# Two half-row stores in place of three stores for the last row block, with its first half scaled by two engines side by side

## Chip, cores, metric

One core of one Trainium2 chip. The metric is the device time of one execution, in microseconds (us). Every ratio below is the mean time of one kernel's fast runs over the mean of the other's fast runs of the same rounds, so it is not quite the ratio of the medians that are quoted. A run is fast when it is within 1.5% of the fastest run of the same kernel. The sets of experiments ran on different chips; a ratio compares runs of one set.

## The reference

```python
m, k, n = 2048, 2048, 2048
def reference(a, b, gamma, eps):
    x = np.matmul(a, b)
    rms = np.sqrt(np.mean(x ** 2, axis=-1, keepdims=True) + eps)
    return (gamma * x / rms).astype(np.float32)
```

The output is 2048 rows of 8 KB. A row can only be scaled when all of it is known, so the last block of 128 rows has a serial end: last matmul, square, root, reciprocal, scale, store.

## The kernel before

The product is computed with a Strassen-like scheme (seven products of half blocks) in 16-bit types. What matters here is the end of the last group of two row blocks, `ra` and `rb`. CH is 512 columns (a quarter of a row, 2 KB), HALF is 1024 (4 KB). `by_r` is a ScalarE ACTIVATE with a scale per row, `scaled_gamma` a VectorE operation.

```python
# ... ra: left quarter by ScalarE, second quarter by GpSimd, right half by VectorE; three stores on nc.sync
right = a_pool.tile([P, K], FP32, name="a32")[:, 0:HALF]
add(right[:, 0:CH], p4[1], gam[2], ALU.mult)
# ... last matmuls into two half banks, their squares, the partial sums
r_b = inverse_rms(half_sq[:, 1:2], part)                       # root on ScalarE, reciprocal on VectorE
nc.vector.tensor_scalar_mul(out=xb[:, 0:CH], in0=xb[:, 0:CH], scalar1=r_b)   # left quarter
nc.sync.dma_start(out=rows(rb, 0, CH), in_=xb[:, 0:CH])
by_r(right[:, 0:CH], r_b)                                      # third quarter
for bank, col in zip(half, halves):
    scaled_gamma(right[:, CH:][:, col], bank, r_b, gam[3][:, col])   # fourth quarter
nc.sync.dma_start(out=rows(rb, HALF, N), in_=right)
by_r(xb[:, CH:], r_b)                                          # second quarter
nc.scalar.dma_start(out=rows(rb, CH, HALF), in_=xb[:, CH:])
```

## Time and profile before

| | |
|---|---|
| time, first three runs | 221.2 us (221.19 to 221.22) |
| profiled span | 219.0 us |
| TensorE busy | 208.8 us, 95% |
| last reciprocal starts | 212.89 us |
| stores of the last block: issue, landing after that start | 0.71, 3.30; 1.53, 4.84; 1.56, 5.01 us |
| from that start to the end ("tail") | 6.11 us |

The lines themselves stand in the prediction. Read them from the end backwards: a closing of 1.1 us, in front of it the landing of the last store, in front of that the bytes. I use the start of the last reciprocal as zero for everything that follows it, since the change can only act after it. A DMA issue is counted from the start of its instruction on the queue; the store "lands" when its semaphore is complete. The time from issue to first packet is called lead, from last packet to landing receipt, from last landing to the end closing. Times of first packets, last packets and landings to a hundredth are read from the trace's packet and semaphore records; the views give landings to a tenth.

### The profile page before, as it was taken

How to read it: one execution, taken by the hardware profiler on the slowest of the kernel's cores; microseconds unless marked ns; L12 is line 12 of the kernel's file. 1: busy time of each engine (PE TensorE's matmuls, PEld its weight loads, DVE VectorE, ACT ScalarE, POOL GpSimd, SP SyncE). 2: the span in 40 equal slices, each digit the busy share in tenths (PEclk: the TensorE clock that was granted, in tenths of full speed). 3: DMA queues.
4: the chain of work that ended last, by engine and by line, in shares of the span. 5: the costliest groups of instructions: out<-in, count | busy, mean ns of one | idle time of the engine just before them, and what ended most of it. 6: DMA issues, size and time to landing. Idle time of an engine off the chain costs nothing.

```text
span 219.0 us, 3023 instructions
## 1 busy us (share of the span) xinstructions
PE 208.8 (95%) x1012; PEld 98.4 (45%) x1032; DVE 165.9 (76%) x326; ACT 127.0 (58%) x263; POOL 36.2 (17%) x75
## 2 busy tenths in 40 slices
PE   7999999999999999999999999999999999999970
PEld 3544544444455444444444444444444444444440
DVE  1228799999899998988794649856794759787781
ACT  2110002920599898788646996289747996334471
POOL 7644433433020002100200002000200000000040
PEclk9999999999999999999999999999999999999996
DMA  7999999999939698939899049955799349145045
GB/s 152 175 202 206 204 206 209 210 208 224 414 91 332 232 278 214 379 153 263 213 294 381 19 87 272 355 233 96 174 291 396 57 89 365 69 178 208 1 179 206
DMA packets 36864, 46.60 MB, mean 213 GB/s; under 512 B 22256, under 2 KB 26352, under 8 KB 35568
## 3 DMA queue, kind: packets, MB, share of 16 engines
q0 software_dynamic: 10608, 23.86, 44.3%
q1 hardware_dynamic: 25824, 22.02, 33.4%
q10 hardware_dynamic: 416, 0.52, 0.7%
q8 instruction: 8, 0.13, 0.2%
q14 instruction: 8, 0.07, 0.1%
HBM read 34.60 MB, written 16.78 MB: 235 GB/s over the span
## 4 chain that ended last, share of the span: by engine, by line
PE 91%; DMA 3%; issue 1%; ACT 1%; POOL 1%; DVE 0%; ACTq 0%; POOLq 0%
PE acc L285 71%; PE acc L388 16%; DMA early<-in_a_dram 3%; PE tbank L419 2%; PE tbank L168 2%; PE acc L799 1%; POOL b L102 0%; PE tbank L185 0%; PE acc L185 0%; ACT x L738 0%; DVE head_at L173 0%; ACT sq L802 0%; ACT rms L352 0%; POOL t_left masks.py:199 0%; POOL t_left masks.py:197 0%
## 5 line engine op out<-in xcount | busy, mean ns | idle before, releaser
L285 PE MATMUL acc<-b,s 128*128 128x512 bf16 x397 | 92.7, 379 | 0.7
L285 PEld LDWEIGHTS <-s 128*128 128x128 f16 (+1 forms) x512 | 50.0, 98 | 59.6 <-DVE s L260 0.2
L388 PE MATMUL acc<-b,head_at 128*128 128x512 bf16 x171 | 42.2, 379 | 0.4 <-DMA b<-in_b_dram 0.3
L303 ACT ACTIVATE sq<-x 128x512 bf16<-128x512 f32 x53 | 33.4, 630 | 6.9 <-DVE x L731 3.0
L370 DVE SCALAR_TENSOR_TENSOR x<-x,r,gamma_sb 128x1024 f32<-128x1024 f32 x28 | 34.9, 1281 | 0.7
L219 ACT ACTIVATE sq<-a 128x1024 bf16<-128x1024 f32 x24 | 25.3, 1053 | 2.0 <-DMA a<-in_a_dram 1.4
L388 PEld LDWEIGHTS <-head_at 128*128 128x128 bf16 x176 | 16.9, 98 | 19.5 <-issue 0.7
L242 ACT ACTIVATE head_at<-a,s 128x2048 f16<-128x2048 f32 x10 | 20.0, 1998 | 3.4 <-DVE s L229 3.3
L102 POOL DMA_DIRECT2D b<-in_b_dram x32 | 17.2, 540 | 20.4 <-DMA b<-in_b_dram 14.1
L430 ACT COPY x<-acc 128x512 f32<-128x512 f32 x5 | 2.9, 582 | 24.6 <-PE acc L388 24.6
L285 PEld LDWEIGHTS <-head_at 128*128 128x128 f16 (+1 forms) x112 | 11.0, 98 | 13.2
L285 PEld LDWEIGHTS <-at_even 128*128 128x128 f16 x96 | 9.4, 98 | 11.3
L285 PE MATMUL acc<-early,head_at 128*128 128x512 bf16 x63 | 14.4, 379 | 0.1
L285 PE MATMUL acc<-early,s 128*128 128x512 bf16 x56 | 14.2, 379 | 0.0
L260 DVE TENSOR_TENSOR s<-head_at 128x1024 f16<-128x1024 f16 (+5 forms) x22 | 13.4, 636 | 0.1
L615 DVE TENSOR_TENSOR x<-x,x 128x512 f32<-128x512 f32 x9 | 6.2, 692 | 8.8 <-ACT x L613 8.3
L127 POOL COPY pace<-x 128x1 f32<-128x1 f32 x4 | 1.7, 413 | 66.3 <-DVE x L624 65.0
L597 ACT COPY x<-acc 128x512 f32<-128x512 f32 x9 | 5.2, 573 | 11.5 <-PE acc L285 7.7
L285 PE MATMUL acc<-t_left,s 128*128 128x512 bf16 x47 | 11.3, 379 | 0.1
L783 POOL TENSOR_SCALAR x<-x,r 128x512 f32<-128x512 f32 x1 | 2.7, 2653 | 51.2 <-DVE r L346 51.2
L276 DVE TENSOR_TENSOR b<-b 128x1024 bf16<-128x1024 bf16 x16 | 10.8, 686 | 0.2
L173 DVE COPY head_at<-tbank 128x1024 bf16<-128x1024 bf16 x7 | 4.8, 692 | 8.0 <-PE tbank L168 7.9
(113 smaller groups left out, 239.3 us busy)
## 6 DMA issues: line engine op xcount, KB each, us to landing
out_dram<-x SPq DMA_DIRECT2D x29, 512.0 KB, 3.7
a<-in_a_dram POOLq DMA_DIRECT2D x10, 1024.0 KB, 8.6
b<-in_b_dram POOLq DMA_DIRECT2D x32, 256.0 KB, 9.9
a<-in_a_dram POOLq DMA_DIRECT2D x4, 512.0 KB, 9.8
early<-in_a_dram POOLq DMA_DIRECT2D x7, 256.0 KB, 10.0
gamma_sb<-in_gamma_dram POOLq DMA_DIRECT2D x2, 512.0 KB, 8.3
out_dram<-x SPq DMA_DIRECT2D x3, 256.0 KB, 2.6
out_dram<-a SPq DMA_DIRECT2D x1, 512.0 KB, 3.3
```

Source lines behind the costliest of these rows:

```text
L102: nc.gpsimd.dma_start(out=raw[j][kp][:, t, :], in_=b[lo:lo + P, j * HALF:(j + 1) * HALF])
L173: nc.vector.tensor_copy(out=head_at[:, 2 * kp:2 * kp + 2, :, :], in_=view)
L219: nc.scalar.activation(out=junk, in_=a32[mb][:, h * HALF:(h + 1) * HALF], func=ACTF.Square, scale=2.0 ** -8, accum_out=n2[:, h:h + 1])
L242: nc.scalar.activation(out=a16[mb], in_=a32.pop(mb), func=ACTF.Copy, scale=factor.pop(mb))
L260: nc.vector.tensor_tensor(out=sum_of(g, s)[:, lo:hi, :], in0=x[:, lo:hi, :], in1=y[:, lo:hi, :], op=op)
L276: nc.vector.tensor_tensor(out=flat[:, 1:3, :], in0=flat[:, 1:3, :], in1=flat[:, 0::3, :], op=ALU.add)
L285: nc.tensor.matmul(bank, lhsT[:, kp, :], rhs, start=(start and kp == 0), stop=(kp == KP - 1), skip_group_check=not start)
L303: nc.scalar.activation(out=sq[:, 0:CH], in_=src, func=ACTF.Square, scale=inv_sqrt_n, accum_out=msq[mb][:, c:c + 1])
L370: nc.vector.scalar_tensor_tensor(out=x, in0=x, scalar=inverse_of[mb], in1=gamma_sb[:, h * HALF:(h + 1) * HALF], op0=ALU.mult, op1=ALU.mult)
L388: nc.tensor.matmul(bank, head_at[:, kt, r, :], head_rhs(c, kt), start=(kt == 0), stop=(kt == KT - 1))
L597: nc.scalar.copy(out=c, in_=one[1])
L615: nc.vector.tensor_tensor(out=t, in0=t, in1=x12, op=ALU.add)
```

## The change

The intent is fewer, larger stores: the left half is finished by two engines at once and goes out as one store of 512 KB, and ScalarE issues no store.

```diff
         nc.vector.tensor_scalar_mul(out=xb[:, 0:CH], in0=xb[:, 0:CH], scalar1=r_b)
-        nc.sync.dma_start(out=rows(rb, 0, CH), in_=xb[:, 0:CH])
+        by_r(xb[:, CH:], r_b)
+        nc.sync.dma_start(out=rows(rb, 0, HALF), in_=xb)
         by_r(right[:, 0:CH], r_b)
         for bank, col in zip(half, halves):
             scaled_gamma(right[:, CH:][:, col], bank, r_b, gam[3][:, col])
         nc.sync.dma_start(out=rows(rb, HALF, N), in_=right)
-        by_r(xb[:, CH:], r_b)
-        nc.scalar.dma_start(out=rows(rb, CH, HALF), in_=xb[:, CH:])
```

## The prediction

> **What bounds the kernel now.** I read the page first (busy shares, then the chain that ended last), then the chain after 208 us, the timeline of the last 6 us, the list of transfers with their landing times, and the DMA rate in quarter microseconds.
>
> ```profile
> PE 208.8 (95%) x1012; PEld 98.4 (45%) x1032; DVE 165.9 (76%) x326; ACT 127.0 (58%) x263; POOL 36.2 (17%) x75
> PE 91%; DMA 3%; issue 1%; ACT 1%; POOL 1%; DVE 0%; ACTq 0%; POOLq 0%
> ```
>
> Matmuls bound the kernel: TensorE is busy for 208.8 of 219.0 us and is 91% of the chain. The change touches nothing that feeds TensorE, so only the time after the last matmul is in play. The chain after 208 us says where that is; its columns are start, length, what:
>
> ```profile
> 210.21 1.76 PE acc L799 x16
> ...
> 212.89 0.17 DVE r L346
> 213.06 0.02 issue
> 213.08 0.03 ACT a L738
> 213.11 0.60 issue
> 213.71 0.70 ACT x L738
> ```
>
> TensorE ends at 211.97. The square, the root and the reciprocal bring 1/rms of the last row block at 213.06. From there to the end, 219.0, is 5.9 us, 2.7% of the span: all that the change can reach, and most of that is a floor. The timeline of that stretch (start, length, engine, line):
>
> ```profile
> 213.08 0.72 ACT L738 ACTIVATE a<-a,r 128x512 f32<-128x512 f32 x1 [0.23 <-DVE r L346]
> 213.09 0.49 DVE L808 TENSOR_SCALAR x<-x,r 128x512 f32<-128x512 f32 x1
> 213.49 0.87 DVE L734 SCALAR_TENSOR_TENSOR a<-acc,r,gamma_sb 128x256 f32<-128x256 f32 x2
> 213.60 0.33 SPq L809 DMA_DIRECT2D out_dram<-x  x1
> 213.71 0.70 ACT L738 ACTIVATE x<-x,r 128x512 f32<-128x512 f32 x1
> 214.42 0.33 SPq L813 DMA_DIRECT2D out_dram<-a  x1
> 214.45 0.36 ACTq L815 DMA_DIRECT2D out_dram<-x  x1
> ```
>
> Three stores leave: 256 KB of the left quarter at 213.60 and, nearly together, 512 KB of the right half at 214.42 (SyncE's queue) and 256 KB of the second quarter at 214.45 (ScalarE's queue). Their times to landing:
>
> ```profile
> out_dram<-a SPq DMA_DIRECT2D x1, 512.0 KB, 3.3
> out_dram<-x ACTq DMA_DIRECT2D x1, 256.0 KB, 3.5
> ```
>
> So the right half lands at 214.42 + 3.3 = 217.7, and the quarter on ScalarE's queue last, at 214.45 + 3.5 = 217.9. The remaining 1.1 us to 219.0 is the closing of the program. What sets 217.9? The DMA rate by quarter microseconds (the last two figures of a row are DMA share and GB/s):
>
> ```profile
> 213.75:214.00 0.25, 0.00 (x0) 0.00 (x0) 0.25 (x2) 0.25 (x2) 0.00 (x0) 1.00 0.10 25
> 214.00:214.25 0.25, 0.00 (x0) 0.00 (x0) 0.25 (x1) 0.25 (x1) 0.00 (x0) 1.00 0.06 16
> 214.25:214.50 0.25, 0.00 (x0) 0.00 (x0) 0.11 (x1) 0.17 (x1) 0.00 (x0) 1.00 0.24 90
> 214.50:214.75 0.25, 0.00 (x0) 0.00 (x0) 0.00 (x0) 0.00 (x0) 0.00 (x0) 1.00 0.99 377
> ...
> 215.00:215.25 0.25, 0.00 (x0) 0.00 (x0) 0.00 (x0) 0.00 (x0) 0.00 (x0) 0.50 0.66 205
> 215.25:215.50 0.25, 0.00 (x0) 0.00 (x0) 0.00 (x0) 0.00 (x0) 0.00 (x0) 0.50 1.08 426
> ```
>
> The engines idle near 214.0 (the block before is out), start at about 214.44 (0.24 of the quarter), and then run full until 217.4, but for one hole: in 215.00 to 215.25 they move 205 GB/s where about 390 would fit, which loses about 0.12 us. There the first 256 KB are out and the next two stores, issued 0.8 us after it, have not begun. So this end is: a first issue, a lead time, 1 MB at the DMA rate, a receipt, the closing. The last ACTIVATE, though the chain names it, is only half of a tie with that queue of bytes.
>
> **What the Trainium skill says.** "DMA: Bandwidth & Descriptors", section "Issuing engines are not separate DMA queues": transfers from SyncE and ScalarE run on the same 16 DMA engines and interleave; a second issuer saves only issue time. The trace agrees: the two stores issued together land within 0.2 us of each other, at one engine set's rate. So dropping ScalarE's queue should cost no bandwidth. The same page, "Latency and other measured facts", gives about 600 ns to first byte on these queues. The trace shows more: 213.60 to 214.44 is 0.84 us, and the store issued at 210.13 began at 210.96, 0.83 us. I use 0.83. "ScalarE: Activation LUTs", section "What ACT_TABLE_LOAD costs": 186 ns + 0.833 ns an element, and about 93 ns for a pointer operand; 512 elements with a pointer scale come to about 706 ns. The trace has 705 to 723 ns.
>
> **The change part by part.**
> - *ScalarE's order.* It scales the second quarter first and the right half's first quarter second. Same two instructions, same lengths: the second quarter is ready at 213.08 + 0.72 = 213.80, the other at about 214.42. No work is added or removed. The built program confirms that only these two change places and one DMA issue goes.
> - *First store.* It is now 512 KB and waits for both engines: VectorE is done at 213.58, ScalarE at 213.80. With the 0.03 us from a ScalarE end to the issue (210.10 to 210.13 for the block before), it goes at 213.83 and not 213.60: **+0.23 us** on the path.
> - *Second store.* The right half needs VectorE (213.49 + 0.87 = 214.36) and ScalarE (214.42): issue at about 214.45, 0.03 later than before. Off the path: the first store's bytes occupy the engines until about 214.66 + 1.3 = 215.95, and this one is ready to stream at 214.45 + 0.83 = 215.28. So the hole at 215.0 disappears.
> - *Third store.* Removed from ScalarE's queue; its bytes ride in the first. 1 MB in all, as before.
>
> How fast does one queue move a pair of half-row stores? The kernel before has a clean pair, issued at 193.9 and 195.1 while no loads run; compared with the present end:
>
> ```profile
> 194.70:197.45 2.75, 2.75 (x13) 1.27 (x13) 2.45 (x6) 1.40 (x4) 0.00 (x0) 1.00 0.94 381
> 214.42:217.41 2.99, 0.00 (x0) 0.00 (x0) 0.00 (x0) 0.00 (x0) 0.00 (x0) 0.58 0.92 351
> ```
>
> The same 1.05 MB take 2.75 us there, 2.99 us here: **-0.24 us** if the new pair is like that pair. It may do a little better, as its second store has more time in hand: at the 400 GB/s of full quarters 1.05 MB take 2.62 us, **-0.37**.
>
> Sum: first byte at 213.83 + 0.83 = 214.66; last byte 2.62 to 2.75 later, 217.28 to 217.41 (before: 217.41); receipt as before, 217.9 - 217.4 = 0.5 us; landing at 217.8 to 217.9. The two terms cancel: +0.23 against -0.24 to -0.37. Net 0.0 to -0.14, middle **-0.1 us**. Closing unchanged at 1.1 us. From the median of 221.2 us, that gives **221.1 us**, a ratio of 0.9995.
>
> **The rivals.**
> 1. *The late start is paid in full.* If the rate were the 351 GB/s of the present end, the 0.23 us would stay: 221.4 us. For it: 1 MB has to follow the first issue in any case, and the idle stretch before it just grows. Against it: the hole at 215.0, which only exists because the first store is short, and the clean pair's 381 GB/s.
> 2. *Fewer issues and one queue bring a real gain.* The old last landing came from ScalarE's queue. If that queue began late and dragged the end, and the receipt shrinks too (the clean pair's second store landed 2.7 us after issue at 195.08, so about 0.35 us after its last byte, against 0.5 here), another 0.15 us goes: 220.9 us. For it: ScalarE's quarter takes 3.5 us to land although it is half the size. Against it: the right half landed only 0.2 us earlier, so the queue can't be blamed for more.
> 3. *A straggler.* Not every late half-row store is clean: of the next pair, issued at 197.5 and 198.7, one took 2.7 and the other 3.4 us to land with no load beside it. A last store that meets this ends 0.7 us late: 221.8 us. For: it happened in one of four such stores. Against: the present three repeats lie within 0.03 us, so it isn't random from run to run, but a changed end may have its own.
>
> None reaches 2%, which is 4.4 us; even all 5.9 us after 1/rms would have to shrink by three quarters.
>
> **Range and chances.** The mechanisms span 220.9 to 221.4 with 221.8 as a tail; repeats differ by 0.03 us, and I allow for another chip or day. Predicted 221.1 us, range 220.8 to 221.5. Within 2%: 0.98; faster by over 2%: 0.01; slower: 0.01.
>
> **What would show it.** In the changed profile: two ACTIVATEs of about 0.71 us back to back from 1/rms, the second quarter first; the first 512 KB store issued about 0.77 us after 1/rms (before: 0.54), the second about 0.62 us after the first; DMA idle until about 1.6 us after 1/rms, then no hole, about 380 to 400 GB/s for some 2.7 us; landings of about 2.7 us for the first and 3.4 us for the second (217.85 - 214.45); a closing of 1.1 us. TensorE and everything before 213 us stay as they are. I am wrong if the hole stays, if the pair runs at 350 GB/s or less, if ScalarE delays the first issue beyond 213.9, or if time moves before the last matmul.

## The result, and the profile after

The changed kernel took 220.87 us (median of 6, 220.70 to 221.83), the kernel before 221.18 us (median of 6, 220.88 to 221.22). The ratio is 0.9995, with a 95% interval of 0.9977 to 1.0013: the same, as far as times can tell. Both spans of the two profiles print as 219.0 us, but their last reciprocals start 0.13 us apart, so the tails differ.

The chain of the changed kernel after the last reciprocal (start, length, what):

```profile
213.02 0.17 DVE r L346
213.20 0.02 issue
213.22 0.72 ACT x L738
213.94 0.61 ACTq L849
```

Two ACTIVATEs in a row ended the old chain. Now the chain names one, then ScalarE's queue at L849, the program's end: it drains until 214.55, when the second ACTIVATE (213.85 + 0.70) is over. So that ACTIVATE still runs; in neither kernel does the chain go on to the transfers. The timeline of the same stretch:

```profile
213.22 0.72 ACT L738 ACTIVATE x<-x,r 128x512 f32<-128x512 f32 x1 [0.23 <-DVE r L346]
213.22 0.49 DVE L808 TENSOR_SCALAR x<-x,r 128x512 f32<-128x512 f32 x1
213.62 0.87 DVE L734 SCALAR_TENSOR_TENSOR a<-acc,r,gamma_sb 128x256 f32<-128x256 f32 x2
213.85 0.70 ACT L738 ACTIVATE a<-a,r 128x512 f32<-128x512 f32 x1
213.97 0.33 SPq L810 DMA_DIRECT2D out_dram<-x  x1
214.58 0.33 SPq L814 DMA_DIRECT2D out_dram<-a  x1
```

The work is the same in the other order. The first store leaves 0.95 us after the reciprocal's start, not 0.71; the second at 1.56. Their landings:

```profile
out_dram<-x SPq DMA_DIRECT2D x1, 512.0 KB, 2.7
out_dram<-a SPq DMA_DIRECT2D x1, 512.0 KB, 3.3
```

And the DMA rate, in two quarter microseconds and over the whole of the two stores (last figures: share, GB/s):

```profile
214.75:215.00 0.25, 0.00 (x0) 0.00 (x0) 0.00 (x0) 0.00 (x0) 0.00 (x0) 1.00 0.94 377
215.00:215.25 0.25, 0.00 (x0) 0.00 (x0) 0.00 (x0) 0.00 (x0) 0.00 (x0) 1.00 0.96 393
```
```profile
214.80:217.55 2.75, 0.00 (x0) 0.00 (x0) 0.00 (x0) 0.00 (x0) 0.00 (x0) 0.89 0.95 380
```

The hole is gone: 1.05 MB take 2.76 us, not 2.98. The last packet ends 4.53 us after the reciprocal's start, in before 4.52. The last store lands at 4.88, in before 5.01. So the first issue costs 0.23 (0.946 against 0.712 unrounded), the bytes give 0.22 back, and the receipt after the last packet falls from 0.49 to 0.35 us. The closing is 1.10 us in both, and the tail 5.98 us, 0.13 less.

### The profile page after: what moved, and what is told of

Same layout as the page of the kernel before. It is cut to its first block, busy times and chain, and to the rows that moved or that the text cites. A ratio compares the mean times of both kernels' runs of the same rounds, so it can differ in the third digit from the quotient of the medians.

```text
span 219.0 us, 3041 instructions
## 1 busy us (share of the span) xinstructions
PE 209.3 (96%) x1032; PEld 97.9 (45%) x1032; DVE 165.9 (76%) x326; ACT 126.9 (58%) x263; POOL 36.4 (17%) x75
## 4 chain that ended last, share of the span: by engine, by line
PE 92%; DMA 3%; ACT 1%; POOL 1%; issue 1%; DVE 0%; ACTq 0%; POOLq 0%
PE acc L285 71%; PE acc L388 16%; DMA early<-in_a_dram 3%; PE tbank L419 2%; PE tbank L168 2%; PE acc L799 1%; POOL b L102 0%; PE tbank L185 0%; PE acc L185 0%; ACT x L738 0%; DVE head_at L173 0%; ACTq L849 0%; ACT sq L802 0%; ACT rms L352 0%; POOL t_left masks.py:199 0%
## 5 line engine op out<-in xcount | busy, mean ns | idle before, releaser
L388 PE MATMUL acc<-b,head_at 128*128 128x512 bf16 x176 | 43.0, 379 | 0.9 <-DMA b<-in_b_dram 0.8
```

The source lines that it names most:

```text
L388: nc.tensor.matmul(bank, head_at[:, kt, r, :], head_rhs(c, kt), start=(kt == 0), stop=(kt == KT - 1))
```

## The experiments

Theory after the result: the end of this kernel is first issue, 0.83 us of lead, 1 MB at about 380 GB/s, a receipt, 1.1 us of closing. Rivals: the 0.13 us is scatter between profiles; it comes from having one queue; it comes from having fewer stores; or the last issue, not the first, sets the end. All edits are against the changed kernel, except where one says otherwise.

All tails, in us after the start of the last reciprocal:

| kernel | first issue | first packet | last packet ends | last landing | tail | median time | ratio to before (95%) |
|---|---|---|---|---|---|---|---|
| before | 0.71 | 1.54 | 4.52 | 5.01 | 6.11 | 221.18 | |
| before again | 0.71 | 1.55 | 4.51 | 5.00 | 6.09 | 221.19 | 1.0003 (0.9983 to 1.0023) |
| changed | 0.95 | 1.77 | 4.53 | 4.88 | 5.98 | 220.87 | 0.9995 (0.9977 to 1.0013) |
| changed again | 0.95 | 1.78 | 4.53 | 4.87 | 5.96 | 220.94 | 0.9991 (0.9969 to 1.0013) |
| third store on SyncE | 0.71 | 1.55 | 4.50 | 5.30 | 6.34 | 221.30 | 0.9999 (0.9984 to 1.0015) |
| three early stores | 0.71 | 1.54 | 4.74 | 5.22 | 6.27 | 221.11 | 0.9991 (0.9975 to 1.0008) |
| left half late | 1.56 | 2.39 | 5.15 | 5.50 | 6.58 | 221.53 | 1.0009 (0.9994 to 1.0024) |
| right half by ScalarE | 0.95 | 1.77 | 4.53 | 4.88 | 5.97 | 221.46 | 1.0010 (0.9962 to 1.0058) |
| right half in 2 KB runs | 0.95 | 1.77 | 4.62 | 4.96 | 6.06 | 221.14 | 1.0008 (0.9976 to 1.0040) |
| left half by rows | 0.95 | 2.15 | 6.58 | 6.91 | 7.96 | 222.97 | 1.0078 (1.0057 to 1.0099) |
| uneven split | 0.84 | 1.67 | 4.42 | 4.77 | 5.86 | 220.87 | 0.9983 (0.9965 to 1.0002) |
| three early, packed in HBM | 0.72 | 1.55 | 4.38 | 4.73 | 5.78 | 220.50 | 0.9958 (0.9921 to 0.9994) |
| one more store | 0.95 | 1.78 | 5.81 | 6.18 | 7.21 | 222.45 | 1.0043 (1.0011 to 1.0075) |
| three early, other block | 0.71 | 1.54 | 4.90 | 5.39 | 6.44 | 221.07 (1 run) | |

The times cannot carry these differences. Over these 14 profiles the last reciprocal starts anywhere from 212.83 to 213.66 us, with the same program up to there (but for one tile's layout in one run): 0.8 us of scatter before the stretch in question, six times the effect. The tails can: each of the two kernels that were profiled twice has the same tail within 0.02 us. The closing is 1.03 to 1.10 us, so differences of tails and of landings can part by up to 0.07 us.

**The changed kernel again** (no edit).

> The changed kernel again, as a control. Tail means the time from the start of the last reciprocal to the end of the span: 6.11 us in the profile of before (212.89 to 218.99), 5.98 us in that of the changed kernel (213.02 to 219.00). My theory (first issue + lead 0.83 + 1 MB without a hole + receipt + closing): tail 5.98 again within 0.05, and a time 0.0 to 0.3 us under before's. Rival 'chance' (the 0.13 us is scatter between profiles): tail anywhere between 5.9 and 6.2.

Tail 5.96 us, so the 0.13 us is no chance. The time ratio is 0.9991, its interval spans 1.

**Before again** (no edit).

> The kernel before again, as a control for its own profile and times. If its tail (from the start of the last reciprocal to the end of the span) is a fixed quantity it is 6.11 us again within 0.05, with landings 3.30, 4.84 and 5.01 us after the reciprocal's start. If its two queues race, as its wider times in the last call suggest (220.77 to 221.80), the last landing moves by 0.1 to 0.4 us.

Tail 6.09, landings 3.29, 4.83 and 5.00: fixed too. The rate over its three stores, by the same view as above:

```profile
214.80:217.77 2.97, 0.00 (x0) 0.00 (x0) 0.00 (x0) 0.00 (x0) 0.00 (x0) 0.72 0.92 353
```

The two queues do not race in these two profiles, and the spread of its times (220.77 to 222.07 over the two sets of rounds that timed it eleven times each) comes from elsewhere.

**Third store on SyncE's queue** (against before):

```diff
-        nc.scalar.dma_start(out=rows(rb, CH, HALF), in_=xb[:, CH:])
+        nc.sync.dma_start(out=rows(rb, CH, HALF), in_=xb[:, CH:])
```

> The kernel before with one word changed: the second quarter is stored on SyncE's queue behind the right half, not on ScalarE's. Nothing issues earlier, and the hole after the first 256 KB stays. Theory 'hole' (the change gains by closing the hole alone): tail 6.11 as before, within 0.05. Rival 'second queue' (two queues running side by side leave a ragged end, 352, 320 and 49 GB/s in the last three quarters of before, against 410, 377 and 197 in the changed kernel): 0.1 to 0.2 us less, tail 5.9 to 6.0, with the last store landing about 3.0 us after its issue at about 1.9 us after the reciprocal's start.

Neither. The last packet ended at 4.50, as in before, but the landing came 0.80 us after it, not 0.49, and the tail grew to 6.34. Dropping ScalarE's queue is not a gain in itself; by itself it lost 0.23 to 0.25 us. Among the last block's stores in these traces (the two that move the place in HBM, below, left aside), a quarter-row store (128 runs of 2 KB) that goes out while the other queue is idle lands 0.78 to 0.97 us after its last packet, a half-row store 0.33 to 0.48. In before, the second quarter and the right half run through the DMA engines side by side, and there the quarter takes 0.49 and the right half 0.54 to 0.56.

**Three early stores:**

```diff
         nc.vector.tensor_scalar_mul(out=xb[:, 0:CH], in0=xb[:, 0:CH], scalar1=r_b)
+        nc.sync.dma_start(out=rows(rb, 0, CH), in_=xb[:, 0:CH])
         by_r(xb[:, CH:], r_b)
-        nc.sync.dma_start(out=rows(rb, 0, HALF), in_=xb)
+        nc.sync.dma_start(out=rows(rb, CH, HALF), in_=xb[:, CH:])
```

> The changed kernel's order on ScalarE, but the left quarter is stored by itself as soon as VectorE has it, so three stores on SyncE's queue, issued about 0.71, 1.08 and 1.56 us after the reciprocal's start. Theory: the first issue comes 0.23 us earlier than in the changed kernel and the second quarter's bytes are there before the first run out, so no hole: first byte at 1.54, last at about 4.2, landing at 4.65, tail 5.75 (0.23 us under the changed kernel, 0.36 under before); time about 220.6 to 220.8. Rival 'fewer stores gain by themselves' (each store costs the engines something, an issue or a completion): tail no better than 5.98, perhaps 6.1. Rival 'something else sets the end': 5.98.

A miss, by half a microsecond: 6.27. The first packet came at 1.54 as expected and there was no hole at first, but then the DMA engines slowed down. The rate from 2.3 to 3.8 us after the reciprocal's start:

```profile
215.39:216.89 1.50, 0.00 (x0) 0.00 (x0) 0.00 (x0) 0.00 (x0) 0.00 (x0) 1.00 1.06 332
```

The engines are counted as fully busy (1.06) while they move 332 GB/s. So two quarter-row stores without a pause after them cost something that the theory had no term for. It could be the number or the size of the stores, the length of a run, or where the runs lie. The next experiments part these.

**Left half late** (the two ACTIVATEs in the order of before):

```diff
         nc.vector.tensor_scalar_mul(out=xb[:, 0:CH], in0=xb[:, 0:CH], scalar1=r_b)
+        by_r(right[:, 0:CH], r_b)
         by_r(xb[:, CH:], r_b)
         nc.sync.dma_start(out=rows(rb, 0, HALF), in_=xb)
-        by_r(right[:, 0:CH], r_b)
```

> The changed kernel with the two scalings on ScalarE in the order of before: the right half's quarter first. The 512 KB store then waits 0.62 us longer (issue about 1.56 us after the reciprocal's start, not 0.95), with the right half behind it at about 1.93. Theory (the first issue is on the path, one for one; 1 MB follows it): tail 5.98 + 0.62 = 6.60 us; time 0.5 us over before's. Rival 'the start is hidden' (the later store or its receipt sets the end, issued only 0.37 us later than in the changed kernel): tail 6.2 to 6.35.

Tail 6.58, against 6.60 expected. The first issue is on the path one for one, and the order on ScalarE is the part of the change that must be kept. Only with that order does the two-store form beat before by its tail.

**Right half by ScalarE's queue:**

```diff
-        nc.sync.dma_start(out=rows(rb, HALF, N), in_=right)
+        nc.scalar.dma_start(out=rows(rb, HALF, N), in_=right)
```

> The changed kernel with its second store, the right half, on ScalarE's queue. Theory (all queues feed the same engines, and a queue's lead is hidden behind the first store's bytes): first byte, rate, landings and tail as in the changed kernel, 5.97 within 0.06. Rival 'ScalarE's queue starts late' (in before its first packet came 1.23 us after the issue, 0.4 us later than on SyncE's queue): the packets of the right half begin 1.23 us after issue, which is still before the first store's bytes run out at about 3.1 us, so no more than 0.05 either; if ScalarE's queue also brings a longer receipt, 0.1 us more, tail 6.05 to 6.1.

Tail 5.97, landings at 3.60 and 4.88 as on one queue. The queue costs nothing and gives nothing.

**Right half in runs of 2 KB** (one store of 512 KB from a tile with a gap between its two quarters):

```diff
-        right = a_pool.tile([P, K], FP32, name="a32")[:, 0:HALF]
+        right = a_pool.tile([P, K], FP32, name="a32").rearrange("p (c n) -> p c n", c=2)[:, :, 0:CH]
 ...     # the uses of right follow
-        nc.sync.dma_start(out=rows(rb, HALF, N), in_=right)
+        nc.sync.dma_start(out=rows(rb, HALF, N).rearrange("p (c n) -> p c n", c=2), in_=right)
```

> The changed kernel, with the right half kept in a tile with a gap in it, so that the same one store of 512 KB is made of runs of 2 KB and not of 4 KB. The stores so far show that those of 2 KB runs land 0.78 to 0.94 us after the engines took up their last packet, those of 4 KB runs 0.35 to 0.42. Theory 'run length' (what counts is the length of a run): the last landing comes at least 0.43 us later, 5.3 us or more after the reciprocal's start and not 4.87, tail 6.4 or more; time 0.3 us over before's. Rival 'number of stores' (a store of 256 KB is slow because it is a store): nothing changes, tail 5.97.

My theory fell: 6.06, not 6.4. The trace has 256 packets of 2 KB as intended, and they take 0.09 us more in all, but the receipt stays at 0.35 us. A run of 2 KB as such is not slow to be written. In this store two runs lie side by side in HBM, though.

**Left half by rows** (two stores of 64 rows, 4 KB runs):

```diff
-        nc.sync.dma_start(out=rows(rb, 0, HALF), in_=xb)
+        nc.sync.dma_start(out=out[rb * P + 0:rb * P + 64, 0:HALF], in_=xb[0:64, :])
+        nc.sync.dma_start(out=out[rb * P + 64:rb * P + 128, 0:HALF], in_=xb[64:128, :])
```

> The changed kernel with its first store cut in two by rows: rows 0 to 63 and rows 64 to 127 of the block, 256 KB each, all runs 4 KB long, both behind the same waits as the one store. So three stores, as in the three-early experiment, but no short run. Theory 'run length': the first part lands about 2.9 us after the reciprocal's start, its lag about 0.4; the last store as before, landing 4.87, tail 5.97 within 0.06. Rival 'number of stores': lags of 0.8 and a tail of 6.2 to 6.3, as in the three-early experiment.

Tail 7.96: both expectations missed, since the cut brought a cost of its own. The rate in two whole microseconds:

```profile
216.00:217.00 1.00, 0.00 (x0) 0.00 (x0) 0.00 (x0) 0.00 (x0) 0.00 (x0) 0.50 0.96 197
217.00:218.00 1.00, 0.00 (x0) 0.00 (x0) 0.00 (x0) 0.00 (x0) 0.00 (x0) 0.50 0.98 283
```

197 GB/s is half the rate of the others. The Trainium skill has this ("SBUF — State Buffer", section "Door 1: The DMA port swizzle"): 64 partitions reach 8 of 16 ports, and it gives 196 GB/s for them at 1 MiB. The trace agrees. I had not looked there before the run. The first packet also came 0.37 us later (2.15, not 1.77); no run here shows why. One thing the run does show: all three receipts are 0.33 to 0.38 us, so at this lower rate a small store as such, or a third one, is not slow to be written either.

**Three early stores, packed in HBM** (wrong result: the two quarters go to 32 whole rows each of an early block, so that the 128 runs lie end to end; against the three-early kernel):

```diff
-        nc.sync.dma_start(out=rows(rb, 0, CH), in_=xb[:, 0:CH])
+        nc.sync.dma_start(out=out[0:0+32, :].rearrange("r (c n) -> (r c) n", c=NCH), in_=xb[:, 0:CH])
 ...
-        nc.sync.dma_start(out=rows(rb, CH, HALF), in_=xb[:, CH:])
+        nc.sync.dma_start(out=out[32:32+32, :].rearrange("r (c n) -> (r c) n", c=NCH), in_=xb[:, CH:])
```

> Wrong result on purpose. The three-early kernel, whose first two stores (quarters, 256 KB each, 128 runs of 2 KB) go not to a quarter of 128 rows, 8 KB apart, but to 32 whole rows of an earlier block each, so the 128 runs lie end to end in HBM. Same bytes, same count and size of stores and packets, same issues. Theory 'place in HBM' (runs of 2 KB at a pitch of 8 KB are slow to be written, not short runs or small stores as such; the one store of 2 KB runs that lie in pairs had a lag of only 0.35): lag 0.35 to 0.45 for all three, no fall of the rate to 270 to 350 GB/s after the second quarter, last landing about 4.65, tail about 5.75. Rival 'small stores' : lags of 0.8 to 0.97 and a tail of 6.2 to 6.3, as the three-early kernel has.

Tail 5.78 against 5.75 expected, receipts of 0.35 to 0.36 us, and the rate holds in the same stretch as above, 2.3 to 3.8 us after the reciprocal's start:

```profile
215.96:217.46 1.50, 0.00 (x0) 0.00 (x0) 0.00 (x0) 0.00 (x0) 0.00 (x0) 0.76 1.04 407
```

Same bytes, same packets, same issues within 0.01 us; the place in HBM alone changed, and 0.49 us went.

**Three early stores into the other block at the old pitch** (wrong result, one run; `rows(rb, ...)` becomes `rows(0, ...)` in the two quarter stores of the three-early kernel):

> Wrong result on purpose; a control for the packed experiment. The three-early kernel with its first two stores into the same early row block that the packed one used, but again as 128 runs of 2 KB at a pitch of 8 KB (the left half of rows 0 to 127). Theory 'place in HBM means the pitch': lags of 0.8 to 0.97 again and a tail of 6.2 to 6.3. Rival 'it was the other row block' (rows written long before, or not adjoining the right half's rows that follow): lags of 0.35 to 0.45 and a tail of about 5.78.

Tail 6.44, receipts of 0.84 and 1.01 us for the two quarters, and again in the same stretch

```profile
215.13:216.63 1.50, 0.00 (x0) 0.00 (x0) 0.00 (x0) 0.00 (x0) 0.00 (x0) 0.88 1.08 325
```

So it was not the other block. A store of 2 KB runs that begin 8 KB apart (a pitch of 8 KB) is slow to be written. The width of the addresses alone is not it: a half-row store (4 KB runs, the same pitch) reaches over 128 rows too, and with the other queue idle its receipt is 0.33 to 0.49 us. No other pitch than 8 KB and the packed 2 KB was tried. The tail lies a little over the 6.2 to 6.3 expected. Why the pitch matters inside the memory, no run here shows.

**One more store** (wrong result):

```diff
         nc.sync.dma_start(out=rows(rb, HALF, N), in_=right)
+        nc.sync.dma_start(out=rows(0, HALF, N), in_=right)
```

> Wrong result on purpose: the changed kernel with a third store of 512 KB behind the two, the right half again, into an early row block that is overwritten so. Nothing before it changes; it is issued at about 1.95 us after the reciprocal's start. Theory 'bytes' (the end is first byte plus all bytes at about 390 to 400 GB/s plus a receipt): tail 5.97 + 1.3 = 7.3, time about 1.3 us over the changed kernel. Rival 'last issue' (the end is the last issue plus a fixed time to landing of 3.3 us): tail 5.97 + 0.4 = 6.35.

Tail 7.21, 1.24 us more for 512 KB (last packet 1.28 later; 7.3 was expected, the last-issue rival said 6.35). The end is bound by bytes.

**Uneven split**, the version that follows from all this:

```diff
-        nc.vector.tensor_scalar_mul(out=xb[:, 0:CH], in0=xb[:, 0:CH], scalar1=r_b)
-        by_r(xb[:, CH:], r_b)
+        nc.vector.tensor_scalar_mul(out=xb[:, 0:672], in0=xb[:, 0:672], scalar1=r_b)
+        by_r(xb[:, 672:], r_b)
```

> The changed kernel with its first store split unevenly: VectorE scales 672 columns, ScalarE 352, so that both end together. VectorE 0.49 us for 512 columns plus about 0.5 ns a column makes 0.57; ScalarE 0.72 less 160 x 0.833 ns makes 0.59. The first issue comes about 0.13 us earlier, at 0.82 us after the reciprocal's start and not 0.95. Theory (first issue on the path one for one, 1 MB in 4 KB runs behind it): last landing 4.74, tail 5.84; time 0.1 to 0.2 us under the changed kernel. Rival 'the right half sets the end' (its store goes later by VectorE's 0.08 us): tail 5.97 to 6.05.

The timeline shows the two engines ending together:

```profile
213.43 0.59 ACT L738 ACTIVATE x<-x,r 128x352 f32<-128x352 f32 x1 [0.23 <-DVE r L346]
213.44 0.57 DVE L808 TENSOR_SCALAR x<-x,r 128x672 f32<-128x672 f32 x1
...
214.07 0.33 SPq L810 DMA_DIRECT2D out_dram<-x  x1
```

The first issue comes at 0.84 and the tail is 5.86 (expected 0.82 and 5.84): 0.11 us under the changed kernel and 0.24 under before. Its median is 220.87 us against 221.12 for before in the same rounds, ratio 0.9983 (0.9965 to 1.0002). It is the best correct version by its tail; by its times it is not shown to beat either kernel, as its interval just includes 1.

## Why the prediction was right

The time fell into the range, and the verdict was "same", as forecast. Point by point:

- *Nothing before the last matmul changes.* Right. What scatters there (0.8 us over 14 profiles) is enough to account for medians that moved by 0.31 us in the first comparison while the tail moved by 0.13.
- *First store 0.23 us later.* Measured 0.23, and shown to be paid one for one (left half late: 0.61 us of issue, 0.61 us of tail).
- *The hole closes, the bytes take 2.62 to 2.75 us.* Right at the slow edge: 2.75 or 2.76 us. Of the 0.22 us that it gives back, the hole is about 0.14 (168 to 176 GB/s from 2.25 to 2.5 us after the reciprocal's start, with each packet's bytes spread over its time, where some 395 fit) and the 2 KB packets about 0.09 (the 2 KB-run store; the packed kernel has 0.08). The prediction had named 0.12 us of hole only; the rest of its 0.24 came from the comparison with the clean pair, without a reason.
- *Receipt as before, 0.5 us.* This term was wrong: 0.35 us. It is the whole of the net gain, since the two terms that I thought would decide, +0.23 and -0.22, cancel. That -0.13 us came out near the forecast of -0.1 is luck: the forecast expected it from the bytes, and it came from a term put at no change. My second rival had this receipt of 0.35, but put it down to ScalarE's queue. One store moved from that queue made it 0.80, and the right half moved to it left it at 0.35; what made it long, as far as the packed and the old-pitch run of the three-early kernel tell, was the second quarter as a store of 2 KB runs 8 KB apart. No run packed that quarter in before itself.
- *Rival 1, the late start is paid in full:* it is paid, and the faster bytes pay it back; the clean earlier pair at 381 GB/s was the right guide (380).
- *Rival 3, a straggler:* the 3.4 us store of the earlier pair takes 3.4 us again in the changed kernel's trace, so it was no chance event; nothing of the kind struck the end.

What the prediction did not see is that, as far as two runs show, the kernel before was helped by its own arrangement: its quarter-row stores are slow to be written, but a hole follows the first, and the other runs interleaved with the right half. Take either away (third store on SyncE, three early stores) and the tail grows to 6.3 us. The change gains little because it trades a late start for not having those stores.

## What to carry to other kernels

At the end of a kernel count five terms: the first issue of the last burst, its lead, all its bytes at the DMA rate, the receipt, the closing; a byte that is ready earlier helps only if the engines are never left without work behind it. Cutting a store into column pieces to send the first piece sooner can lose more in the writing than it gains in the start, and cutting it by rows can halve its rate. For an effect of a tenth of a microsecond compare tails from a common event in the trace, not times.

## What the Trainium skill lacked or had wrong

- "DMA: Bandwidth & Descriptors", "Latency and other measured facts", has figures for row pitches from 512 KiB up, and none for a small pitch. Here stores of 128 runs of 2 KB at a pitch of 8 KB had receipts of 0.78 to 1.01 us while the other queue was idle, the same runs packed 0.35 to 0.36, and two of them in a row pulled the rate down to 325 to 332 GB/s, from 407.
- The same section's first byte after about 600 ns on these queues: here 0.83 us from issue to the first packet of the burst, in every kernel whose first store has 128 rows, and 1.20 us where it has 64.
